# A hybrid decoder layer on one core: gate weights, gate bias and second norm around the end of the expert loop

## The chip, the cores and the metric

The kernel runs on one core of a Trainium2 chip. The metric is the device time of one execution in microseconds (us). Of three runs of the kernel before, the median is 1200.3 us (1199.73 to 1201.92).

## The reference

For 256 tokens of width 1024 the layer computes a token mixer, a mixture of experts and a gated per-layer embedding:

```
h = layer_norm(ALPHA * x + mixer(x) @ w_out) * ln1_g + ln1_b
m = sum over the top 4 of 32 experts of gate_e * (swiglu(h @ w_up[e] + b_up[e]) @ w_down[e] + b_down[e])
h = layer_norm(ALPHA * h + m) * ln2_g + ln2_b
out = h + sigmoid(h @ w_ple_gate + b_ple_gate) * (p @ w_ple)
```

All of it is in float32, and all 32 experts' weights (12 MB each) are read from HBM.

## The kernel before

The order of all work is written by hand: each engine runs its instructions in the order in which the program issues them, and semaphores hold an instruction until its inputs have landed and its output's place is free.

**Slots.** Most of SBUF is 22 buffers ("slots") of 128 x 2048 float32. `take` pops the first slot of a free list, `give` appends one to it. Weights stream through the slots, 1 MB in each, in one fixed list: for expert e the eight row blocks of `w_up` (`up`), the four of `w_down` (`dn`) of the expert before in between, `w_ple` (`ple`) in expert 27, and after the last expert the four pieces of `w_ple_gate` (`pg`). SyncE issues these loads (L63) as slots come free. A new tile in a slot waits for everything that used the slot before, the loads of its former tile among them.

**Expert loop** (L1257 on). For each expert and each k of 8, `up_slot` multiplies a 128-row block; at k = 1 the transposes of the expert before (`mid`), at k = 2 its `down`, at k = 4 and 5 of even experts `scatter` adds two experts' results to `z`. Each expert has room for 64 tokens. Tokens beyond that go through `overflow`: a loop over extra blocks whose count is known only at run time, inside `tc.If(n > 0)` (L1104) after the last expert's up matmuls, with its own weight buffer `ov`. In the profiled execution the count is zero, so each engine jumps over the loop. Where it jumps, SyncE passes a row of semaphore events that make good for the loads that the loop would have issued.

**Per-layer embedding.** At the start of expert 27 `late_take` takes three slots (`pp`, `ple`, `gb2`) and loads `p` by GpSimd's queue. At the start of expert 28 `ple_mm` transposes it, lets VectorE copy the transposes (L1040), multiplies it with `w_ple` into `ple` (L1046), and spreads the second norm's scale and shift over all partitions into `gb2` with a matmul each (`bc_row`), copied out by ScalarE.

**After the loop.** `gate_high` rounds the gate weights to fp32r (`pgh`, L1159 on ScalarE and L1161 on GpSimd), `gate_low` makes the remainders (`pgl`, VectorE). The last pair's `scatter` and the second norm are done one 128-token half (t = 0, 1) after the other: `stats2`, `norm2` (a square root on ScalarE, L1180, two small VectorE instructions), `norm2_apply` (`zn`, L1187). `trans2` transposes `zn` and applies scale and shift on ScalarE (`h2h`, `pp`; L1212); `high2` and `low2` split the result. `gate_mm` accumulates high x high, high x low and low x high into five PSUM chunks (two of 512 columns for t = 0; 512, 256 and 256 for t = 1). Each chunk is opened by `gate_start`, a matmul that puts `b_ple_gate` into it: before, from row 67 of `bd` in float32 with four rows (L1229). `scale2` applies scale and shift to the residual copy (GpSimd for t = 0, VectorE for t = 1), and `finish` does sigmoid, product, sum and output for a chunk.

Of the kernel before, what the change touches and what calls it, by code (L numbers as in the profile page):

```python
# [10 lines left out]
BF = mybir.dt.bfloat16  # L11
# [3 lines left out]
OP = mybir.AluOpType  # L15
# [32 lines left out]
class Stream:  # L48
# [25 lines left out]
    def give(self, *names, keep=0):  # L74

        self.slots.keep += keep
        for name in names:
            self.slots.free.append(self.slots.held.pop(name))
        self.pump()
# [3 lines left out]
def hybrid_layer(ctx, tc, x, p, w_in, conv_w, conv_b, lru_w_r, lru_b_r, lru_w_i, lru_b_i, lru_lambda,  # L83
# [55 lines left out]
    iota32 = cp.tile([128, NE], F32, name="iota32")  # L139
    tri = cp.tile([128, 128], F32, name="tri")  # L140
    one = cp.tile([128, 1], F32, name="one")
    epsc = cp.tile([128, 1], F32, name="epsc")
    fold = cp.tile([128, NE], F32, name="fold")
    foldb = cp.tile([128, NE], BF, name="foldb")
# [28 lines left out]
    V.memset(one, 1.0)  # L173
    ones = one.to_broadcast([128, 128])
    V.memset(epsc, EPS)
    V.memset(wglr, 0.0)
    G.memset(wgt, 0.0)
    make_identity(nc, ident)
# [850 lines left out]
    def late_take():  # L1029
        late["pp"] = take("pp", (2, 4, T))  # L1030
        late["ple"], late["gb2"] = take("ple", (2, D)), take("gb2", (2, D))
        G.dma_start(late["pp"][:, 0, 0:2], p[0, 0].rearrange("(t p) c -> p t c", p=128))  # L1032

    def ple_mm():
        ple, gb2, pt2, pTt = late["ple"], late["gb2"], late["pp"][:, 0, 0:2], late["pp"][:, 1, 0:2]
        o = pt("b", [128, 2, T], "ppT")
        for kk in range(2):
            for t in range(2):
                PE.transpose(o[:, kk, t * 128:(t + 1) * 128], pt2[:, t, kk * 128:(kk + 1) * 128], ident)
        V.tensor_copy(pTt, o)  # L1040
        w = st.get(("ple", 0))
        for t in range(2):
            for dh in range(2):
                o = pt("c", [128, 512], "pl")
                for kk in range(2):
                    PE.matmul(o, lhsT=pTt[:, kk, t * 128:(t + 1) * 128], rhs=w[:, kk, dh * 512:(dh + 1) * 512], start=(kk == 0), stop=(kk == 1))  # L1046
                A.activation(ple[:, t, dh * 512:(dh + 1) * 512], o, AF.Copy)
        st.done(("ple", 0))
        for r in range(2):
            for dh in range(2):  # L1050
                A.activation(gb2[:, r, dh * 512:(dh + 1) * 512], bc_row(1 + r, dh), AF.Copy)
# [43 lines left out]
    def overflow(n):  # L1095
        ov = take("ov", (2, 1024))
        ctr = mw.tile([128, 1], F32, name="ctr")
        sc = mw.tile([128, 8], F32, name="osc")
        V.memset(ctr, -1.0)

        def dot(a, o):
            V.scalar_tensor_tensor(tmo, a, 1.0, sel, op0=OP.mult, op1=OP.mult, accum_out=o)

        with tc.If(n > 0):  # L1104
            with tc.For_i(0, n, 1):
                V.tensor_scalar(ctr, ctr, 1.0, None, op0=OP.add)
                V.tensor_scalar(sel, sta, ctr, None, op0=OP.is_le)
                V.scalar_tensor_tensor(sel, cum, ctr, sel, op0=OP.is_gt, op1=OP.mult)
                dot(iota32, sc[:, 0:1])
                V.tensor_copy(ti[:, 1:2], sc[0:1, 0:1])  # L1110
                er = nc.values_load(ti[0:1, 1:2], min_val=0, max_val=NE - 1, engines=[mybir.EngineType.SP])
                dot(sta, sc[:, 1:2])
                V.tensor_tensor(sc[:, 1:2], ctr, sc[:, 1:2], op=OP.subtract)
                V.tensor_scalar(sc[:, 1:2], sc[:, 1:2], 64.0, 64.0, op0=OP.mult, op1=OP.add)
                for t in range(2):
                    dot(posb[:, t, :], sc[:, 2 + t:3 + t])
                    V.tensor_tensor(sc[:, 2 + t:3 + t], sc[:, 2 + t:3 + t], sc[:, 1:2], op=OP.subtract)
                    dot(gate[:, t, :], sc[:, 4 + t:5 + t])
                dot(fold, sc[:, 6:7])
                selb = mw.tile([128, C], BF, name="selb")  # L1120
                V.tensor_copy(selb, sc[:, 6:7].to_broadcast([128, C]))
                oh = mw.tile([128, 2, 4, C], F32, name="oh", tag="oh")[:, :, 0]
                for t in range(2):
                    V.tensor_scalar(oh[:, t], iota64[:, 0, :], sc[:, 2 + t:3 + t], None, op0=OP.is_equal)
                xo = ov[:, 1, 0:512].rearrange("p (k c) -> p k c", k=KD)
                for k in range(KD):
                    gather_k(oh[:, :, None, :], xo, 0, k)
                gu = up_start(selb, "b")

                def wload(src):  # L1130
                    w = ov[:, 0]
                    SP.dma_start(w, src)
                    return w

                for k in range(KD):
                    for a in range(2):
                        w = wload(w_up[0, bass.ds(er, 1), k * 128:(k + 1) * 128, a * 1024:(a + 1) * 1024].rearrange("o p c -> p (o c)"))
                        up_mm(gu, xo[:, k, :], w, k == KD - 1, (a,))
                aT = act_T(swiglu(gu, mo2), mo2)
                se = scatter_mat(lambda i, t: (sc[:, 2 + t:3 + t], sc[:, 4 + t:5 + t]),  # L1140
                                 mw.tile([128, 4, T], F32, name="x1", tag="x1")[:, 0])
                o = pt("b", [128, 512], "dn")
                dnv = w_down[0].rearrange("e (q p j) c -> e q j p c", p=128, j=2)
                for q in range(4):
                    for j in range(2):
                        w = wload(dnv[bass.ds(er, 1), q, j].rearrange("o p c -> p (o c)"))
                        down_mm(o, aT, q, w.rearrange("p (j c) -> p j c", j=1), (j,))
                y_evac(o, 1)
                for t in range(2):
                    scatter(se, t, slice(64, 128))  # L1150
        give("ov")

    def gate_high(i, *ens):

# [18 lines left out]
    def stats2(t):  # L1173
        for hf in range(2):
            stats(z, sb2, t, hf)
        V.bn_aggr(mv2[:, t, 0:2], sb2[:, t, :, :])
# [49 lines left out]
    def gate_start(tag, *chunks):  # L1226
        for t, c0, c1 in chunks:
            o = pgs[t, c0, c1] = pt(tag, [128, c1 - c0], "pg")
            PE.matmul(o, lhsT=ident[64:68, 67:68].to_broadcast([4, 128]), rhs=bd[64:68, c0:c1], start=True, stop=False)  # L1229

    def gate_mm(i, j, *chunks):

# [22 lines left out]
    for e in range(NE):  # L1255
        g = e // 4
        for k in range(KD):  # L1257
            if k == 0:
                if e == 8:
                    z_init()  # L1260
                if e == PLE - 1:
                    late_take()
                if e == PLE:
                    ple_mm()

            if (e, k) in ((0, 6), (0, 7), (2, 2)):
                hold(1)
            if k == 4 and e == PLE - 2:
                hold(3)
            if k == 7 and e % 4 == 2 and e < NE - 4:  # L1270
                hold(1)
            if (e, k) == (0, KD - 1):
                mo = take("mo", (4, 512))
            if (e, k) == (2, 4):
                z = take("z", (2, D))
            up_slot(e, k)
            if e == 0 and k == 1:
                gates()
            if e and e % 2 == 0 and k in (4, 5):
                scatter(PAIR[e // 2 - 1], k - 4, first=(e == 2))  # L1280
            if e and k == 1:
                mid(e - 1, mo)
            if e and k == 2 and e < NE - 1:
                down(e - 1)
            if (e, k) == (NE - 1, 5):
                gate_start("a", *c0)
            if (e, k) == (9, 6):
                blocks = overflow_count()
            if e == 0 and k < KD - 2:
                gather_k(oh, x1[0], 0, k + 2, 2)  # L1290
            if e == 1:
                if k == 0:
                    x1.append(take("x1b", (2, KD, 2 * C))[:, 0])
                gather_k(oh, x1[1], 2, k, 2)
            if e % 4 == 3 and e < NE - 1:
                if k == 0:
                    oh = gather_start(g + 1)
                if k % 2:
                    gather_mm(oh, XE[g + 1], k // 2)
            if e % 4 == 3 and k == KD - 1:  # L1300
                give(f"xe{g}" if g else "x1b")
# [19 lines left out]
    norm2(0)  # L1321
    norm2_apply(0)
    scatter(PAIR[NE // 2 - 1], 1)
    gate_start("a", *c1[:2])
    gate_start("c", c1[2])
    stats2(1)
    trans2(0)
    whole2(0, 0)
    high2(0, 1)
# [20 lines left out]
    gate_mm(1, 0, *c1)  # L1350
    dump("z", z)
    scale2(1, 0, V)
    for n, c in enumerate(c0):
        gate_mm(0, 1, c)
        finish(n, *c)
    scale2(1, 1, V)
    for n, c in enumerate(c1):
        gate_mm(0, 1, c)
        finish((2 + n) % 4, *c)
# [30 lines left out]
```

## Time and profile before

| | |
|---|---|
| median of three runs | 1200.3 us |
| profiled execution, its own time | 1197.4 us |
| its span in the trace | 1195.7 us |
| TensorE busy | 1137.6 us (95%) |
| VectorE busy | 410.8 us (34%) |
| ScalarE busy | 250.8 us (21%) |
| GpSimd busy | 36.9 us (3%) |
| read from HBM | 445 MB, 373 GB/s over the span |

Times in the trace count from the span's start; PE is TensorE, DVE VectorE, ACT ScalarE, POOL GpSimd, SP SyncE, and a q behind an engine's name means its sequencer or DMA queue. In a timeline a row merges instructions of one kind that follow each other: start, time from the first one's start to the last one's end, engine, line, operation, output<-input, shapes and count; in brackets the idle time of the engine before it and what ended that. [...]

### The profile page before, as it was taken

To read this page: it belongs to the slowest core of one execution; us is meant where nothing else is said; L and a number is where in the kernel's file an instruction comes from. 1 tells how busy PE (TensorE), PEld (TensorE's weight loads), DVE (VectorE), ACT (ScalarE), POOL (GpSimd) and SP (SyncE) were. 2 spreads that over 40 slices of the span, in tenths; PEclk is the share of its full clock that TensorE was granted. 3 is DMA by queue.
4 is the path that set the end of the run, shared out by engine and by line. 5 is a ranking of instruction groups with operands and counts; after the bars stand their busy time and mean duration, and the time that the engine had idled before them with its cause. 6 is when DMAs were issued, how large, how long until landed. Compare 5 with 4: busy or idle time off the path is not lost. (4 is left out here: it accounts for less than half of the span.)

```text
span 1195.7 us, 14336 instructions
## 1 busy us (share of the span) xinstructions
PE 1137.6 (95%) x5886; PEld 550.4 (46%) x5886; DVE 410.8 (34%) x717; ACT 250.8 (21%) x404; POOL 36.9 (3%) x66
## 2 busy tenths in 40 slices
PE   8999999999999999999999988998899889999888
PEld 7999999643343343334333322332233223333236
DVE  8589687621212223231212121211121112121227
ACT  5784664411010010001000100100010001200033
POOL 6000000000000000000000000000000000000020
PEclk9999999999999998999999999999999999999988
DMA  9654865899999999999999999999999999999960
GB/s 337 218 168 143 278 252 205 351 352 421 414 426 426 427 426 427 426 426 427 426 426 427 426 428 426 427 426 427 427 426 427 427 426 426 427 427 427 426 268 36
DMA packets 92849, 447.16 MB, mean 374 GB/s; under 512 B 9345, under 2 KB 40423, under 8 KB 43532
## 3 DMA queue, kind: packets, MB, share of 16 engines
q1 hardware_dynamic: 91008, 444.69, 90.7%
q10 hardware_dynamic: 1340, 1.10, 0.4%
q8 instruction: 47, 0.77, 0.2%
q0 software_dynamic: 432, 0.42, 0.1%
q14 instruction: 22, 0.18, 0.0%
HBM read 445.13 MB, written 1.05 MB: 373 GB/s over the span
## 5 line engine op out<-in xcount | busy, mean ns | idle before, releaser
L935 PE MATMUL gu<-up,xe 128*64 128x512 f32 x1792 | 417.9, 602 | 17.6 <-DMA up<-in_w_up_dram 17.3
L962 PE MATMUL dn<-dn,mo 128*64 128x512 f32 x1024 | 232.3, 598 | 16.3 <-DMA dn<-in_w_down_dram 12.4
L935 PEld LDWEIGHTS gu<-up,xe 128*64 128x64 f32 x1792 | 119.5, 137 | 268.7 <-issue 202.0
L971 DVE COPY y2b<-dn 64x512 f32<-64x512 f32 x32 | 22.2, 694 | 391.8 <-ACT mo L973 391.8
L962 PEld LDWEIGHTS dn<-dn,mo 128*64 128x64 f32 x1024 | 71.7, 137 | 171.8 <-issue 134.3
L943 ACT ACTIVATE mo<-mo 128x512 f32<-128x512 f32 x32 | 20.1, 630 | 299.3 <-DVE mo L942 299.3
L973 ACT ACTIVATE mo<-dn 64x512 f32<-64x512 f32 x32 | 18.9, 591 | 267.9 <-PE dn L962 267.9
L999 DVE TENSOR_TENSOR z<-z,sc 128x512 f32<-128x512 f32 x60 | 41.2, 688 | 89.9 <-PE sc L995 89.9
L942 DVE TENSOR_SCALAR mo<-gu 128x512 f32<-128x512 f32 x32 | 22.1, 692 | 130.9 <-PE gu L935 112.2
L915 PE MATMUL ga<-oh,X 128*128 128x256 f32 x224 | 55.1, 389 | 0.0
L955 ACT ACTIVATE mo<-aTp 128x512 f32<-128x512 f32 x32 | 19.1, 598 | 150.9 <-PE aTp L954 150.9
L915 PEld LDWEIGHTS ga<-oh,X 128*128 128x128 f32 x224 | 40.3, 190 | 21.4 <-issue 8.1
L995 PE MATMUL sc<-mo,se 128*128 128x512 f32 x64 | 36.0, 645 | 0.7 <-ACT mo L973 0.7
L920 DVE TENSOR_SCALAR xe<-ga,parTB 128x256 f32<-128x256 f32 x28 | 15.2, 543 | 60.0 <-PE ga L915 60.0
L995 PE MATMUL sc<-y2b,se 128*128 128x512 f32 x64 | 32.7, 592 | 0.0
L918 ACT ACTIVATE xe<-ga,parTB 128x256 f32<-128x256 f32 x28 | 15.8, 565 | 74.8 <-PE ga L915 74.8
L935 PE MATMUL gu<-up,x 128*64 128x512 f32 x128 | 30.7, 603 | 0.0
L954 PEld LDWEIGHTS aTp<-ident,mo 128*128 128x128 f32 x128 | 17.7, 207 | 26.0 <-issue 25.2
L935 PE MATMUL gu<-up,x1b 128*64 128x512 f32 x128 | 29.5, 597 | 0.0
L293 PE MATMUL acc<-wo,yhl 128*128 128x512 f32 x96 | 23.5, 398 | 0.8 <-DVE wo L262 0.8
L1032 POOL DMA_DIRECT2D pp<-in_p_dram x1 | 0.8, 842 | 746.4 <-DMA up<-in_w_up_dram 746.4
L944 DVE TENSOR_SCALAR mo<-gu 128x512 f32<-128x512 f32 x32 | 22.1, 691 | 5.2 <-PE gu L935 5.2
(340 smaller groups left out, 1195.3 us busy)
## 6 DMA issues: line engine op xcount, KB each, us to landing
up<-in_w_up_dram SPq DMA_DIRECT2D x256, 1024.0 KB
dn<-in_w_down_dram SPq DMA_DIRECT2D x128, 1024.0 KB
v<-in_w_in_dram SPq DMA_DIRECT2D x4, 1024.0 KB
ma<-in_w_in_dram SPq DMA_DIRECT2D x4, 1024.0 KB
ga<-in_w_in_dram SPq DMA_DIRECT2D x4, 1024.0 KB
go<-in_w_in_dram SPq DMA_DIRECT2D x4, 1024.0 KB
mb<-in_w_in_dram SPq DMA_DIRECT2D x4, 1024.0 KB
wo<-in_w_out_dram SPq DMA_DIRECT2D x4, 1024.0 KB
```

The source lines that it names most:

```text
L293: PE.matmul(o, lhsT=l(k)[i], rhs=r(k)[j], start=first and m == 0, stop=last and m == len(n) - 1)
L915: PE.matmul(o, lhsT=X[:, t, k * 128:(k + 1) * 128], rhs=oh[:, t], start=(t == 0), stop=(t == 1))
L935: PE.matmul(gu[a][64 * hf:64 * hf + 64, :], lhsT=xk, rhs=w[:, (a - parts[0]) * 1024 + hf * 512:(a - parts[0]) * 1024 + hf * 512 + 512], st ...
L942: V.tensor_scalar(gc, gu[0], LIM, None, op0=OP.min)
L943: A.activation(sg, gc, AF.Sigmoid, scale=1.702)
L944: V.tensor_scalar(uc, gu[1], LIM, -LIM, op0=OP.min, op1=OP.max)
L955: A.activation(aT, o, AF.Copy)
L962: PE.matmul(o[64 * dh:64 * dh + 64, :], lhsT=aT[:, 2 * c + j, hf * 64:hf * 64 + 64], rhs=w[:, j - js[0], dh * 512:(dh + 1) * 512], start=( ...
L971: V.tensor_copy(dst, src)
L973: A.activation(dst, src, AF.Copy)
L995: PE.matmul(o, lhsT=se[rows, t * 128:(t + 1) * 128], rhs=(y2b if dh else mo[:, 3])[rows], start=True, stop=True)
L999: V.tensor_tensor(z[:, t, dh * 512:(dh + 1) * 512], z[:, t, dh * 512:(dh + 1) * 512], o, op=OP.add)
```

## The change

- `overflow` no longer gives `ov` back, so no later tile takes that slot.
- The gate bias is loaded by GpSimd's queue in `late_take` into partitions 0, 64 and 96 of a zeroed `gb2`. In expert 28, ahead of `ple_mm`, `gate_bias` makes three bfloat16 parts of it there: ScalarE rounds, VectorE subtracts the rounded part in the partitions from 64 (from 96) on, ScalarE rounds the rest. They stay in an unused part of the slot `pp`.
- `gate_start` becomes a bfloat16 matmul of ones (128 rows) with these parts.
- The first two gate starts move from expert 31 (k = 5) to after the last scatter. Eight matmuls of 128x256 on a buffer of zeros (`spin`) follow them, and the last gate start comes behind `stats2(1)`.
- `scale2(1, 1)` moves ahead of the first `finish`.

```diff
+    oneb = cp.tile([128, 1], BF, name="oneb")
...
+    V.memset(oneb, 1.0)
...
         G.dma_start(late["pp"][:, 0, 0:2], p[0, 0].rearrange("(t p) c -> p t c", p=128))
+        G.memset(late["gb2"], 0.0)
+        for i in (0, 64, 96):
+            G.dma_start(late["gb2"][i:i + 1, 0], b_ple_gate)
+
+    def gate_bias(n):
+
+        b, h = late["gb2"][:, 0], late["pp"][:, 0, 2:4].rearrange("p a b -> p (a b)").bitcast(BF)
+        late["pgb"] = h
+        if n == 0:
+            A.activation(h, b, AF.Copy)
+        else:
+            r = slice((0, 64, 96)[n], 128)
+            V.tensor_tensor(b[r], b[r], h[r], op=OP.subtract)
+            A.activation(h[r], b[r], AF.Copy)
...
                 for t in range(2):
                     scatter(se, t, slice(64, 128))
-        give("ov")
...
-            PE.matmul(o, lhsT=ident[64:68, 67:68].to_broadcast([4, 128]), rhs=bd[64:68, c0:c1], start=True, stop=False)
+            PE.matmul(o, lhsT=oneb.to_broadcast([128, 128]), rhs=late["pgb"][:, c0:c1], start=True, stop=False)
...
                 if e == PLE:
+                    for n in range(3):
+                        gate_bias(n)
                     ple_mm()
...
-            if (e, k) == (NE - 1, 5):
-                gate_start("a", *c0)
...
     scatter(PAIR[NE // 2 - 1], 1)
-    gate_start("a", *c1[:2])
+    gate_start("a", *c0, *c1[:2])
+    spin(8, "b")
+    stats2(1)
     gate_start("c", c1[2])
-    stats2(1)
...
     scale2(1, 0, V)
+    scale2(1, 1, V)
     for n, c in enumerate(c0):
         gate_mm(0, 1, c)
         finish(n, *c)
-    scale2(1, 1, V)
```

The order on ScalarE after the last expert's result is evacuated (`mo<-dn`), before, with the semaphores that each instruction waits for (HW0 to HW7 are the queues of SyncE's loads in turn; `pg_0` is on HW6, `pg_3` on HW1):

```order
L973 ACTIVATE mo_2838<-dn_6597 64x512 [waits PE_49]
L1159 ACTIVATE pgh0_6619<-pg_0_6315 128x1024 [waits DMAHW4_49,DMAHW6_49,DMAHW3_49,DMAHW1_49]
L1159 ACTIVATE pgh0_6619<-pg_0_6315 128x1024
L1159 ACTIVATE pgh1_6623<-pg_1_6321 128x1024 [waits DMAHW7_49,DMAHW0_49]
L1180 ACTIVATE mv2_2745<-mv2_2745,epsc_77 128x1 [waits DVE_49]
L1187 ACTIVATE zn_6618<-z_3044,mv2_2745 128x512 [waits DVE_49]
```

and in the changed kernel:

```order
L975 ACTIVATE mo_2840<-dn_6604 64x512 [waits PE_49]
L1174 ACTIVATE pgh0_6626<-pg_0_6326 128x1024 [waits DMAHW7_49,DMAHW6_49,DMAHW4_49]
L1174 ACTIVATE pgh0_6626<-pg_0_6326 128x1024
L1174 ACTIVATE pgh1_6630<-pg_1_6332 128x1024 [waits DMAHW7_49,DMAHW0_49]
L1195 ACTIVATE mv2_2747<-mv2_2747,epsc_78 128x1 [waits DVE_49]
L1202 ACTIVATE zn_6625<-z_3046,mv2_2747 128x512 [waits DVE_49]
```

The order of instructions is the same; the list of semaphores of the first copy has changed, since its output now lies in another slot.

The order on VectorE at the turn from expert 27 to 28, before (`gu` are the up results, `xe` the last gathered tokens, `ppT` the transposed embedding):

```order
L942 TENSOR_SCALAR mo<-gu_5819 128x512 [waits PE_49]
L944 TENSOR_SCALAR mo<-gu_5820 128x512 [waits DVE_49,PE_49]
L945 SCALAR_TENSOR_TENSOR mo<-mo 128x512 [waits DVE_49]
L946 TENSOR_TENSOR mo<-mo 128x512 [waits DVE_49,Activation_49]
L920 TENSOR_SCALAR xe_5834<-ga,parTB 128x256 [waits PE_49]
L1040 COPY pp<-ppT 128x512 [waits DMAHW4_49,DMAHW3_49,DMAHW6_49,DMAHW1_49,PE_49]
```

and in the changed kernel:

```order
L947 SCALAR_TENSOR_TENSOR mo<-mo 128x512 [waits DVE_49]
L948 TENSOR_TENSOR mo<-mo 128x512 [waits DVE_49,Activation_49]
L922 TENSOR_SCALAR xe_5840<-ga,parTB 128x256 [waits PE_49]
L1047 TENSOR_TENSOR gb_5819<-gb_5819,pp 64x1024 [waits DMAHW0_49,DMAHW3_49,DMASW6_49,DMAHW6_49,DMASW5_49,Activation_49]
L1047 TENSOR_TENSOR gb_5819<-gb_5819,pp 32x1024 [waits Activation_49]
L1056 COPY pp<-ppT 128x512 [waits DMAHW4_49,DMAHW6_49,DMAHW1_49,PE_49]
```

Two subtractions stand ahead of the copy, each behind a rounding on ScalarE. ScalarE's three roundings (L1044 and twice L1048) stand there between its last `xe` and the copies of `ple`.

## Rows read from the trace of the kernel before

**Rows 1.** The page: the busy share of the DMA engines in 40 equal slices

```profile
DMA  9654865899999999999999999999999999999960
```

**Rows 2.** Timeline of ScalarE after the last expert's result

```profile
1151.09 0.59 ACT L973 ACTIVATE mo<-dn 64x512 f32<-64x512 f32 x1 [4.76 <-PE dn L962]
1158.03 2.95 ACT L1159 ACTIVATE pgh<-pg 128x1024 fp32r<-128x1024 f32 x3 [6.35 <-SPq L1104]
...
1161.59 1.52 ACT L1187 ACTIVATE zn<-z,mv 128x512 f32<-128x512 f32 x2 [0.42 <-DVE mv L1182]
1164.51 1.51 ACT L1212 ACTIVATE h2h<-t,parTB 128x128 fp32r<-128x128 f32 x4 [1.40 <-PE t L1209]
```

**Rows 3.** Line 1104 by engine: count, ns min/median/max, first and last start

```profile
L1104 SPq EVENT_SEMAPHORE  x9: 17/17/17, 1146.1 to 1158.4; - x9
...
L1104 PEldq COMPARE_BRANCH  x1: 5802/5802/5802, 1128.4 to 1128.4; - x1
```

**Rows 4.** Timeline of GpSimd after the last expert's result

```profile
1153.17 1.03 POOL L1161 CAST pgh<-pg 128x1024 fp32r<-128x1024 f32 x1 [169.92 <-DMA pg<-in_w_ple_gate_dram]
...
1162.49 1.28 POOL L1192 TENSOR_TENSOR z<-zn,gb 128x512 f32<-128x512 f32 x1 [2.37 <-ACT zn L1187]
```

**Rows 5.** Timeline of VectorE after the last expert's result

```profile
1155.67 0.21 DVE L1176 BATCH_NORM_AGGREGATE mv<-sb 128x2 f32<-128x12 f32 x1
...
1167.44 0.54 DVE L1220 CAST h2h<-pp 128x512 fp32r<-128x512 f32 x1
...
1185.22 0.69 DVE L1241 TENSOR_TENSOR mo<-mo,ple 128x512 f32<-128x512 f32 x1 [1.77 <-ACT mo L1240]
...
1187.83 0.69 DVE L1242 TENSOR_TENSOR z<-z,mo 128x512 f32<-128x512 f32 x1
...
1192.34 0.42 DVE L1242 TENSOR_TENSOR z<-z,mo 128x256 f32<-128x256 f32 x1
```

**Rows 6.** Timeline of TensorE after the last scatter

```profile
1155.56 1.55 PE L1229 MATMUL pg<-bd,ident 4*128 4x512 f32 x4
1162.21 1.22 PE L1229 MATMUL pg<-bd,ident 4*128 4x256 f32 x2 [5.10 <-DVE z L999]
1163.36 1.97 PE L1209 MATMUL t<-ident,zn 128*128 128x128 f32 x8
1165.02 5.62 PE L1235 MATMUL pg<-pgh,h2h 128*128 128x512 f32 x16
1170.47 1.99 PE L1235 MATMUL pg<-pgh,h2l 128*128 128x512 f32 x8
```

**Rows 7.** Busy time by engine in two stretches, granted clock behind it

```profile
1166.00:1168.00 2.00, 2.00 (x6) 1.57 (x5) 1.93 (x6) 1.59 (x6) 1.62 (x2) 0.50 0.00 0
...
1170.00:1175.00 5.00, 5.00 (x27) 4.06 (x26) 3.38 (x5) 2.48 (x7) 0.00 (x0) 1.00 0.00 0
```

**Rows 8.** Timelines in experts 27 and 28; the last row from the DMA issues

```profile
1023.83 7.10 PE L1046 MATMUL pl<-ple,pp 128*128 128x512 f32 x16 [1.05 <-ACT xe L918]
...
1034.58 0.62 PE L862 MATMUL gu<-bub,foldb 128*64 128x512 bf16 x4
...
1023.05 0.68 DVE L1040 COPY pp<-ppT 128x512 f32<-128x512 f32 x1
...
982.40 0.84 POOL L1032 DMA_DIRECT2D pp<-in_p_dram  x1 [746.41 <-DMA up<-in_w_up_dram]
...
pp<-in_p_dram POOLq DMA_DIRECT2D x1, 256.0 KB, 7.2
```

**Rows 9.** TensorE's waits for `up` weights (us, times, longest) after 1096; its timeline

```profile
PE gu L935 <- DMA up<-in_w_up_dram: 1.6, 3, 0.6
...
1125.34 1.98 PE L1229 MATMUL pg<-bd,ident 4*128 4x512 f32 x4
...
1134.67 6.97 PE L962 MATMUL dn<-dn,mo 128*64 128x512 f32 x24 [3.77 <-PEq L1104]
...
1142.24 8.80 PE L962 MATMUL dn<-dn,mo 128*64 128x512 f32 x40
```

## The prediction

> **What bounds the kernel now.** I read the page first, then the chain of waits, then the timeline of one engine after another over the last 45 us, and last the stretch from expert 28 to the end of the expert loop. The page shows the DMA engines full from the ninth slice to the end of that loop [rows 1]: the weight stream sets the pace there, and a stall of TensorE costs only what has not been made up when the stream ends. The chain's only long piece is the gate matmuls close to the end. So the change is worth what it does between the last expert's result and the last output, less what its new work in expert 28 leaves over.
>
> In that stretch ScalarE is free at 1151.09 + 0.59 = 1151.68 and then sits for 6.35 us; its first weight copy (`pgh`, L1159) starts at 1158.03, and the idle time is put down to SyncE at L1104 [rows 2]. L1104 is the `tc.If` of the overflow blocks. SyncE goes through nine semaphore events there, from 1146.1 to 1158.4 [rows 3]: with no overflow block to run it stands in for the loads that it skips, queue after queue, and each event waits for the real loads before it, the gate weights at last. A slot whose last writer is `ov` is free only then. The copy needs none of the later weights: the second of the four had landed at 1153.17, when GpSimd's first cast started [rows 4], and the first stands before it in the stream. Behind the three copies stand the square root of the second norm, at 1158.03 + 2.95 = 1160.98, and `zn` (1161.59) [rows 2]. VectorE had the mean and variance at 1155.67 + 0.21 [rows 5] and TensorE did nothing from 1157.11 to 1162.21 [rows 6].
>
> **The change part by part.** All times are the profiled execution's.
>
> 1. *Slot not given back.* ScalarE's first copy waits for HW7, HW6 and HW4, no longer for HW1 and HW3 (its order is shown with the change); HW6 carries its own weight. Three copies take 2.95 [rows 2]: they run from 1151.7 to 1154.8, the third with a short wait for the second weight. The square root then waits for VectorE's 1155.88 and starts at 1155.9 instead of 1161.0: **-5.0**.
>
> 2. *Gate starts and spin.* [...] Moved by 5.0, `zn` ends at 1158.1. [...] The first four transposes (half of `zn`, from 1157.4) are then done when ScalarE gets free, and `h2h` starts at 1158.15: 6.36 ahead, so **-1.36** (-0.9 at the late end). The cast that opens the second half of the first gate block goes from 1167.44 [rows 5] to 1161.1. [...]
>
> 3. *Second `scale2` sooner.* Before, VectorE idled 1.77 until its first finish at 1185.22; after the second finish's last add (1187.83 + 0.69) it spent 1.3 on `scale2(1,1)` and then worked without a gap to 1192.76 [rows 5]. Now those two instructions of 0.69 fit into the 1.77. The next sigmoid was ready at about 1188.8; three finishes of two instructions each (2 x 0.69, then four of 0.4) end at about 1191.9: **-0.9**.
>
> 4. *Bias parts in expert 28.* They stand ahead of VectorE's copy of `ppT`, for which the `pl` matmuls wait. Before, the copy ran from 1023.05 for 0.68 and `pl` started at 1023.83 after 1.05 of idle time [rows 8]. Now ScalarE, VectorE, ScalarE, VectorE alternate ahead of it, each waiting for the one before: two copies of 1024 columns at 1.0 [rows 2] and two subtractions of 1024 columns, for which 0.69 for 512 [rows 5] gives 0.69 to 1.38. I take 1.3, for 512 columns cost 0.69 in each such row: `pl` starts 4.6 later (bounds 3.4 and 4.8). The bias rows come by GpSimd's queue, a memset and three small loads behind that of `pp`, which was issued at 982.4 and took 7.2 to land [rows 8]; four such one after another end at 1011, so nothing waits for them. An idle time like this also takes the clock down: after 3.77 idle, 24 down matmuls took 6.97, 0.29 each, and 40 later ones 0.22 each [rows 9], 1.7 in all. **Lag 4.6 to 6.3.**
>
> Made up before the loop ends: three waits for weights, 1.6 together, and the two fp32 gate starts in expert 31, 1.98 from 1125.34, which are gone [rows 9]. Left: 1.0 to 2.7. Behind them lies TensorE's jump over the overflow code, 5.80 from 1128.4 [rows 3], for which it idled 3.77 before L962 [rows 9]. If that time runs from when the sequencer reaches the branch, the lag vanishes in it; if it runs from the end of the matmuls, all of it stays. The row leans to the first (the branch began while up matmuls were still to run), but not with more of them queued: bounds 0 and 2.7, I take **+1.2**.
>
> On the branch the trace has that one row. [...]
>
> Sum: -5.0 - 1.36 - 0.67 - 0.9 + 1.2 = **-6.7**. 1197.4 becomes 1190.7; the profiled execution lies 2.9 under the median of the runs, so the forecast is 1200.3 - 6.7 = **1193.6**.
>
> **The rivals.**
>
> *A. GpSimd and VectorE hold each other up.* GpSimd's casts still wait for the weights, so its four `scale2` instructions (1.28 each [rows 4]) start at about 1160.2, 2.3 earlier only, while VectorE's `h2l` and first `pgl` move by 6 to 7, into them. If two or three of the four hold VectorE up for 1.3 each, it is 2.6 to 3.9 late; its wait for ScalarE absorbs 0.9 and the last `pgl` has some 1.4 to spare: about +1.0 to 1.6, so **1195.0**. Against it: a cast beside VectorE's adds from PSUM took its usual 1.03 [rows 4]. For it: no VectorE instruction with two SBUF inputs lay beside a GpSimd one there. [...]
>
> [...]
>
> *C. Expert 28's lag is kept whole.* Were the stream itself held up by late slots, only the gate starts would be won back: 6.3 - 1.9 in place of 1.2, **1196.8**. Against it: the DMA engines stayed full though TensorE spent 1023.8 to 1034.6 [rows 8] on work that frees no weight slot.
>
> *D. The wait is not the slot's.* If the copies are held by something else that ends at 1158, the 0.9 of part 3 and some 1.4 of part 2 stand against 1.2: **1199.2**, no change. The list of semaphores speaks against it.
>
> *E. Slower.* The bias rows land late, because the memset waits for its slot's last reader and the loads for one another, and expert 28 waits for them. The gain of 7.9 and the 3.5 made up cover a lag of 11.4, or 6.3 and a landing 5.1 after 1023; so it decides from 1028, or up to 3.8 later if the branch hides some. A landing at 1032 with nothing hidden: **1204**. Against it: the 1011 of part 4.
>
> **How the numbers follow.** Forecast 0.52 (its own range 1192.0 to 1195.0), A 0.16, B 0.13, C 0.08, D 0.06, E 0.05. A measurement of this kernel tells about 0.2%, 2.4 us, from no change. Faster means below 1197.9, which takes in the forecast, A, B and most of C; D and the rest of C are the same; E is slower: 0.85, 0.10 and 0.05. The range goes down to a lag that costs nothing and the upper ends of parts 2 and 3, 1191.0, and up past C, 1197.8.
>
> **What would show it.** Right: the first `pgh` copy right after ScalarE's last evacuation; the square root at VectorE's statistics; a granted clock of 1.00 through the first gate block; no `scale2` after a finish; `pl` 4 to 5 us later behind `xe`. Wrong: a copy that still waits for SyncE; `pgl` pieces longer than 1.3 or with gaps beside GpSimd; gaps in the DMA stream after expert 28; the down matmuls of expert 30 more than 3 us later.

## The result and the profile after

The changed kernel took 1209.44 us (median of 4 runs, 1209.2 to 1210.81), the kernel before beside it 1200.01 (4 runs, 1198.76 to 1201.92): a ratio of 1.008, 95% interval 1.0062 to 1.0097. It is 9.4 us slower; 6.7 less was forecast. The profiled execution has a span of 1208.0 and a time of 1209.67.

**Where the time went.** The middle of the expert loop first: windows of five experts, cut at ScalarE's evacuation of the down result (`mo<-dn`, the copy of an expert's result out of PSUM; start:end, length, busy time and count of PE, PEld, DVE, ACT, POOL, then the clock granted to TensorE as a share of its full speed, DMA share, GB/s). Before:

```profile
740.03:888.09 148.06, 137.31 (x590) 46.70 (x590) 32.23 (x58) 12.73 (x23) 0.00 (x0) 1.00 1.01 427
```

The same five experts after:

```profile
749.73:900.91 151.18, 137.96 (x590) 46.55 (x590) 32.22 (x58) 12.72 (x23) 0.00 (x0) 1.00 1.01 419
```

The same instructions, the same granted clock (1.00), a full DMA share (1.01) in both, and the last number differs: 427 and 419 GB/s. TensorE's busy time is 0.65 longer; the other 2.5 of the 3.1 us more are idle time, 2.3 of it waits for weights (13.0 against 10.7). An expert's weights are 12 loads of 1 MiB, 12.58 MB: at 427 GB/s 29.5 us, at 419 30.0, and the windows give 29.6 and 30.2. Followed along the loop, the same evacuation is late by 3.2 at the first expert (the runs e1, e5 and e6 below were 1.7 to 1.8 late there, whatever their slots), 4.9 at the fourteenth, 9.7 at the eighteenth, 14.4 at the twenty-seventh and 18.2 at the last. Up to the fourteenth TensorE sets the pace in both. Then the stream takes over in the changed kernel (TensorE is busy for 97% of 600 to 700 us), and after 700 us in the kernel before too (100% of 500 to 700, 91% of 700 to 800). The nine experts from the eighteenth evacuation to the twenty-seventh take 267.0 before and 271.7 after.

Nothing in the diff touches a weight load. What moved is their address. `oneb` is a tile of 2 bytes per partition in the constants pool, where it takes 32 (it lies at 36384, the next tile at 36416), and the pool of weight slots lies right behind: the first slot starts at byte 36864 before (9 x 4096) and at 36896 after, and all that follow it are moved with it. No trace holds an address: those given here and below stand in the built programs.

**The tail.** Timeline of ScalarE after (start, us, engine, line, operation, in brackets the idle time ahead and what ended it), the answer to [rows 2]:

```profile
1169.27 0.59 ACT L975 ACTIVATE mo<-dn 64x512 f32<-64x512 f32 x1 [4.76 <-PE dn L964]
1169.88 2.95 ACT L1174 ACTIVATE pgh<-pg 128x1024 fp32r<-128x1024 f32 x3
1174.10 0.30 ACT L1195 ACTIVATE mv<-mv,epsc 128x1 f32<-128x1 f32 x1 [1.26 <-DVE mv L1191]
1175.46 1.52 ACT L1202 ACTIVATE zn<-z,mv 128x512 f32<-128x512 f32 x2 [1.07 <-DVE mv L1197]
1177.03 1.51 ACT L1227 ACTIVATE h2h<-t,parTB 128x128 fp32r<-128x128 f32 x4
```

The 6.35 us for SyncE are gone; the copies follow the evacuation, and the square root waits for VectorE, as the prediction had it. TensorE, the answer to [rows 6], and its granted clock (third number) in two windows, to [rows 7]:

```profile
1173.64 0.92 PE L1244 MATMUL pg<-pp,oneb 128*128 128x512 bf16 x4
1174.40 1.04 PE L304 MATMUL spin<-bub 128*128 128x256 bf16 x8
1176.08 0.27 PE L1244 MATMUL pg<-pp,oneb 128*128 128x256 bf16 x1 [0.65 <-DVE z L1001]
1176.33 1.36 PE L1224 MATMUL t<-ident,zn 128*128 128x128 f32 x8
1177.54 2.11 PE L1250 MATMUL pg<-pgh,h2h 128*128 128x512 f32 x8
1181.00 2.08 PE L1250 MATMUL pg<-pgh,h2h 128*128 128x512 f32 x8 [1.35 <-DVE h2h L1235]
```

```profile
1174.00:1180.00 6.00, 4.95 (x29) 1.00 0.07 27
1180.00:1186.00 6.00, 4.63 (x22) 1.00 0.01 3
```

VectorE, to [rows 5], and GpSimd, to [rows 4]:

```profile
1179.96 0.89 DVE L1235 CAST h2h<-pp 128x512 fp32r<-128x512 f32 x1
1180.77 1.76 DVE L1238 TENSOR_TENSOR h2l<-pp,h2h 128x512 fp32r<-128x512 f32 x1
1182.46 0.15 DVE L1196 RECIPROCAL mv<-mv 128x1 f32<-128x1 f32 x1
1182.64 1.06 DVE L1197 SCALAR_TENSOR_TENSOR mv<-mv 128x1 f32<-128x1 f32 x1
1183.62 0.68 DVE L1238 TENSOR_TENSOR h2l<-pp,h2h 128x512 fp32r<-128x512 f32 x1
...
1198.38 0.69 DVE L1256 TENSOR_TENSOR mo<-mo,ple 128x512 f32<-128x512 f32 x1 [0.46 <-ACT mo L1255]
...
1204.60 0.42 DVE L1257 TENSOR_TENSOR z<-z,mo 128x256 f32<-128x256 f32 x1
```

```profile
1179.30 1.27 POOL L1208 TENSOR_TENSOR z<-z,gb 128x512 f32<-128x512 f32 x1
1180.52 1.46 POOL L1207 TENSOR_TENSOR z<-zn,gb 128x512 f32<-128x512 f32 x1
1182.06 1.62 POOL L1208 TENSOR_TENSOR z<-z,gb 128x512 f32<-128x512 f32 x1
```

From the last evacuation's start to VectorE's end the tail took 1205.02 - 1169.27 = 35.75, before 41.67: 5.92 won, not the 7.9 of the prediction's parts 1 to 3. The granted clock is 1.00 in both windows. Beside GpSimd's three operations the cast took 0.89, the first h2l 1.76 and the small L1197 1.06; the second h2l, after GpSimd's end, took 0.68.

**Expert 28 and the branch**, to [rows 8, 9 and 3]: the bias parts on ScalarE and VectorE, then TensorE, then the branch over the overflow code (count, ns min/median/max, start).

```profile
1038.09 1.05 ACT L1044 ACTIVATE pp<-gb 128x1024 bf16<-128x1024 f32 x1
1039.17 1.22 DVE L1047 TENSOR_TENSOR gb<-gb,pp 64x1024 f32<-64x1024 f32 x1 [0.79 <-ACT pp L1044]
...
1042.77 0.69 DVE L1056 COPY pp<-ppT 128x512 f32<-128x512 f32 x1
...
1043.56 9.06 PE L1062 MATMUL pl<-ple,pp 128*128 128x512 f32 x16 [5.53 <-issue]
```

```profile
1143.21 1.94 PE L937 MATMUL gu<-up,xe 128*64 128x512 f32 x8 [0.56 <-DMA up<-in_w_up_dram]
1145.71 1.94 PE L937 MATMUL gu<-up,xe 128*64 128x512 f32 x8 [0.56 <-DMA up<-in_w_up_dram]
1152.23 7.58 PE L964 MATMUL dn<-dn,mo 128*64 128x512 f32 x24 [4.59 <-PEq L1120]
```

```profile
L1120 PEldq COMPARE_BRANCH  x1: 6082/6082/6082, 1145.7 to 1145.7; - x1
```

`pl` starts after 5.53 of idle time, 1.05 before, and its matmuls take 1.96 more. Over the 24 down matmuls behind the branch the mean granted clock was 0.70, after 4.59 of idle time; before it was 0.77, after 3.77. TensorE waits for weights again at 1143.21, so it has caught up with the (slower) stream: nothing of the lag is left.

In sum: the last evacuation is 18.18 late, the tail 5.92 shorter, 12.26 in the traces. The profiled execution of before (1197.4) lay 2.6 under the 1200.01 and that of after 0.2 over its median, which leaves the 9.4.

### The profile page after: what moved, and what is told of

It is laid out like the page before. It is cut to its first block, busy times and chain, and to the rows that moved or that the text cites. A ratio compares the mean times of both kernels' runs of the same rounds, so it can differ in the third digit from the quotient of the medians.

```text
span 1208.0 us, 14362 instructions
## 1 busy us (share of the span) xinstructions
PE 1142.4 (95%) x5889; PEld 551.2 (46%) x5889; DVE 416.6 (34%) x720; ACT 254.0 (21%) x407; POOL 39.4 (3%) x70
## 3 DMA queue, kind: packets, MB, share of 16 engines
HBM read 445.14 MB, written 1.05 MB: 369 GB/s over the span
## 5 line engine op out<-in xcount | busy, mean ns | idle before, releaser
L937 PE MATMUL gu<-up,x1b 128*64 128x512 f32 x128 | 29.5, 597 | 0.0
```

What stands on the lines that cost most here:

```text
L937: PE.matmul(gu[a][64 * hf:64 * hf + 64, :], lhsT=xk, rhs=w[:, (a - parts[0]) * 1024 + hf * 512:(a - parts[0]) * 1024 + hf * 512 + 512], st ...
```

## Experiments

Theory T: the 32 bytes by which the weight slots moved slow the stream, and without that the change does about what the prediction's steps say. Rivals: the stream is slower for another reason (the new work in expert 28, the added instructions), and the tail's missing 2 us are the lag's.

**e1, the change with the slots put back.**

```
-    one = cp.tile([128, 1], F32, name="one")
-    oneb = cp.tile([128, 1], BF, name="oneb")
+    one2 = cp.tile([128, 2], F32, name="one")
+    one, oneb = one2[:, 0:1], one2[:, 1:2].bitcast(BF)[:, 0:1]
```

> The changed kernel, with the bfloat16 ones put into the unused bytes behind the float32 one, so that every slot starts again at the SBUF address that it has in the kernel before (36864 + n x 8192; in the changed kernel 32 bytes further). Theory A (the 32 bytes slow the weight stream): the stream is back at 427 GB/s, the up matmuls of expert 31 end as in the kernel before or up to 2.7 us later, and the kernel takes 1193 to 1197. Theory B (something else in the change slows the stream, such as the work of late_take or the slot that is not returned): still 420 GB/s and about 1209.

1193.82 us (1192.95 to 1194.82), ratio 0.9959 (0.9945 to 0.9972); the stream at 427 GB/s. Two names in one tile of the size that `one` had taken turn 9.4 us lost into 4.9 won (before beside it: 1198.7).

**e2, e3, e5, e6: the kernel before, with only the slots moved.** An unused tile ahead of them, of 32 bytes (`cp.tile([128, 8], F32, name="pad")`), of 64, of 128; and, in e6, the 256-byte tile `csb` taken out from ahead of them:

```
-    csb = cp.tile([128, 2, NE], F32, name="csb")
...
+    csb = ctx.enter_context(tc.tile_pool(name="cz", bufs=1)).tile([128, 2, NE], F32, name="csb")
```

> The kernel before with 32 unused bytes ahead of the slots, nothing else. Theory A: 420 GB/s and 1212 to 1218, that is the changed kernel's stream without its gain at the end. Theory B: 1200.

> The kernel before with 64 unused bytes ahead of the slots. If only the remainder modulo 64 counts, 427 GB/s and 1200; if the slots have to start at a multiple of 128 or more, 420 GB/s and 1212 to 1218. Theory B: 1200.

> The kernel before with 128 bytes of padding in the constants pool, unused: the weight slots start at 36992, a multiple of 128 and not of 256. Theory (the slots' start has to be a multiple of 256 bytes for the full rate; 32 bytes off gave 1215.96 us and 420 GB/s, 64 off gave 1212.0 and 421): still slow, 1208 to 1214 us, 419 to 422 GB/s through the experts' loop, 8 KB packets at a median of 312 to 313 ns. Rival (128 is enough): 1199 to 1202 us, 427 GB/s, 309 ns. Rival (the padding itself, or the place in the partition, costs in proportion to the shift): between 1216 and 1225.

> The kernel before with its 256-byte tile csb placed behind the weight slots and not ahead of them: the slots start at 36608, a multiple of 256 and not of 512. Theory (256 bytes): 1198 to 1202 us as before, 427 GB/s, packets at a median of 309 ns. Rival (512 or more is wanted, before and the aligned version both stood at 36864, a multiple of 4096): 1208 to 1216 us, 420 to 422 GB/s.

The packet times are those of the 49,276 packets of 8 KB in each trace (49,277 in e2), median and mean in ns; such a packet is one partition's row of a 1 MiB load.

| slots start at | off by | us | ratio to before | GB/s | packet |
|---|---|---|---|---|---|
| 36864 (before) | 0 | 1200.01 | | 427 | 309, 312.2 |
| 36896 (after) | 32 | 1209.44 | 1.008 (1.0062 to 1.0097) | 419 to 420 | 313, 317.7 |
| 36896 (e2) | 32 | 1215.96 | 1.0134 (1.0115 to 1.0153) | 420 | 313, 317.3 |
| 36928 (e3) | 64 | 1212.0 | 1.0104 (1.0086 to 1.0122) | 421 | 312, 316.5 |
| 36992 (e5) | 128 | 1212.08 | 1.0105 (1.0089 to 1.012) | 421 | 312, 316.3 |
| 36608 (e6) | 256 | 1199.55 | 1.0002 (0.9993 to 1.0012) | 427 | 309, 312.4 |

Windows of e5, and then of e6, over the same stretch:

```profile
700.00:900.00 200.00, 179.74 (x777) 58.71 (x773) 40.01 (x72) 16.63 (x30) 0.00 (x0) 1.00 1.01 421
```

```profile
700.00:900.00 200.00, 183.34 (x794) 61.96 (x792) 38.67 (x71) 17.10 (x31) 0.00 (x0) 1.00 1.01 427
```

The padding alone makes the kernel before slower; 128 bytes off are as bad as 64, and 256 cost nothing, though 36608 is no multiple of 512. So it is where the slots start, not the size of the shift and not the change's own work: 427 GB/s from the two starts that are multiples of 256 (36864 and 36608), 419 to 421 from those 32, 64 or 128 bytes past one, and none of these four kernels has an instruction that the kernel before lacks. The mean packet took 1.3 to 1.8% longer from the latter; what inside the DMA engines costs it no run shows.

**e4, the bias parts in expert 27** (`gate_bias` called at `(e, k) == (PLE - 1, 3)` in e1, not ahead of `ple_mm`).

> As e1_aligned, with the bias parts made in expert 27 at k = 3 instead of ahead of the embedding's matmuls in expert 28. If the lag of expert 28 is made up by the weight stream and hidden under the branch at the end of the loop, the same time as e1_aligned within 0.5 us; if 1 to 2.7 us of it are left, faster by that.

1194.28 us (1193.75 to 1195.65), ratio 0.9963 (0.995 to 0.9977): no different from e1. Without the lag TensorE reaches the branch sooner and idles longer behind it. TensorE in e1, then in e4:

```profile
1125.17 10.52 PE L937 MATMUL gu<-up,xe 128*64 128x512 f32 x48
1137.60 5.37 PE L964 MATMUL dn<-dn,mo 128*64 128x512 f32 x24 [1.91 <-PEq L1120]
```

```profile
1138.26 8.08 PE L964 MATMUL dn<-dn,mo 128*64 128x512 f32 x24 [4.31 <-PEq L1120]
```

In e1 the branch starts at 1131.2, takes 5.92, and runs beside TensorE's last up matmuls. After 1.91 of idle time the 24 down matmuls take 5.37, at a granted clock of 1.00 from 1138 to 1143; after 4.31 they take 8.08, and the clock of the same stretch of e4 is 0.50.

**e10, the slot alone** (the kernel before without `give("ov")`).

> The kernel before with one line of the change alone: the overflow block's slot isn't given back. No tile is added, so the weight slots stay where they were (427 GB/s). Theory (ScalarE's 6.35 us wait for SyncE at L1104 was the slot's, and goes): the first weight copy right after ScalarE's last evacuation, 4 to 5.5 us sooner in the tail; 1194.5 to 1196.0 us. Rival (the wait is another's and stays): 1199 to 1201.

1195.19 us (1194.14 to 1196.39), ratio 0.9965 (0.9952 to 0.9979). ScalarE, TensorE and a window with its granted clock:

```profile
1154.22 0.59 ACT L973 ACTIVATE mo<-dn 64x512 f32<-64x512 f32 x1 [4.76 <-PE dn L962]
1154.83 2.95 ACT L1158 ACTIVATE pgh<-pg 128x1024 fp32r<-128x1024 f32 x3
```

```profile
1160.38 0.69 PE L1228 MATMUL pg<-bd,ident 4*128 4x256 f32 x2 [0.15 <-DVE z L999]
1161.01 1.09 PE L1208 MATMUL t<-ident,zn 128*128 128x128 f32 x8
1162.21 3.45 PE L1234 MATMUL pg<-pgh,h2h 128*128 128x512 f32 x8
1166.34 2.08 PE L1234 MATMUL pg<-pgh,h2h 128*128 128x512 f32 x8 [0.68 <-DVE h2h L1219]
```

```profile
1163.00:1166.00 3.00, 2.67 (x7) 0.50 0.00 0
```

One line brings nearly all: the tail is 36.33 long, 5.34 under before's. (It lasts 41.4 to 42.2 in before, e2, e3, e5 and e6, which share it, and 35.2 to 36.5 in after, e1, e4 and e13; less than about 1 us between two tails shows nothing.)

**e11, e1 without the spins** (`spin(8, "b")` left out).

> The aligned version of the change without the eight spin matmuls ahead of the first transposes. [...] Rival (TensorE comes from the scatter and the gate starts with so little idle time that the clock holds without spins): 1193.3 to 1194.3, granted clock 1.00 over the first gate block.

1194.73 us (1193.24 to 1195.17), ratio 0.9957 (0.9944 to 0.9971), tail 35.75. TensorE and the same window:

```profile
1161.96 2.11 PE L1250 MATMUL pg<-pgh,h2h 128*128 128x512 f32 x8
1164.98 2.08 PE L1250 MATMUL pg<-pgh,h2h 128*128 128x512 f32 x8 [0.91 <-DVE h2h L1235]
```

```profile
1163.00:1166.00 3.00, 2.09 (x10) 1.00 0.03 5
```

Had the spins held the granted clock up, the author's estimate was 1194.6 to 1195.6 without them, and the time alone fits that, but e1 itself, run again as e13, took 1195.01. The trace decides for the rival: without spins the granted clock is 1.00 here, so the spins are worth nothing that can be seen. In e10, behind two four-row fp32 gate starts, the clock fell to 0.50 in this stretch, and the first eight gate matmuls took 3.45; in e11, behind four 128-row bfloat16 ones, it was 1.00, and they took 2.11. Form and number changed together, in one trace of each, so which of them did it is not shown.

**e12, e1 with the last `scale2` back behind the second finish.**

> The aligned version of the change with the last scale2 where it was before, behind the second finish. Theory (the move is worth 0.9 us, because VectorE works without a gap from there to its end): 1194.4 to 1195.2 us, the last VectorE instruction 0.6 to 1.2 later after down(30)'s start. Rival (the finishes wait for TensorE's last matmuls anyway): 1193.5 to 1194.1.

1194.99 us (1194.13 to 1196.26), ratio 0.9962 (0.9949 to 0.9975). In time this can't be told from e1. In the trace it can: from the start of VectorE's last four `pgl` pieces (1176.38) to its end (1191.62) 15.24, in e1 14.37 (1174.59 to 1188.96): 0.87, the prediction's 0.9.

**e7, e8, e9: GpSimd beside VectorE.** e7 is e1 without `scale2(0, 0, G)` and `scale2(0, 1, G)`, so that tokens 0 to 127 leave without the second scale and shift; e8 does them later, held back by a copy that reads VectorE's result; e9 does them on VectorE:

```
     high2(1, 0)
+    G.tensor_copy(warm, h2[0][:, 0, 128:129].bitcast(F32))   # e8
+    scale2(0, 0, G)
+    scale2(0, 1, G)
```

```
+    scale2(0, 0, V)          # e9
     high2(1, 0)
...
+    scale2(0, 1, V)
     scale2(1, 0, V)
     for n, c in enumerate(c0):
         gate_mm(0, 1, c)
         finish(n, *c)
+        if n == 0:
+            scale2(1, 1, V)
```

> The aligned version of the change (1193.82 us) without GpSimd's four operations of the second scale and shift of tokens 0 to 127 (that half of the output leaves unscaled): it prices the pair GpSimd/VectorE. Theory (they hold each other up: VectorE's h2l took 1.78 us beside GpSimd and 0.68 alone, the small L1197 1.06 and not 0.16): h2l back at 0.68, L1197 at 0.16 for t = 1, the second norm's zn about 2 us sooner, the last VectorE instruction 1 to 2 us sooner after down(30)'s start; 1191.5 to 1193.0 us. Rival (what VectorE gains is covered by TensorE and ScalarE): 1193.5 to 1194.2.

> The aligned version of the change with GpSimd's second scale and shift held back until VectorE has made the h2 high part of tokens 128 to 255, by a one-element copy on GpSimd that reads it (some 4.5 us later in the tail, all work kept). Theory: h2l and L1197 at 0.68 and 0.16, zn of t = 1 about 2 us sooner; GpSimd's four operations then stand beside L1182, L1238 and scale2(1) of VectorE and lengthen these, partly under TensorE's last 64 matmuls: 1192.0 to 1193.6 us, at best the time without the four operations. Rival (the cost only moves: VectorE is late for the last matmuls or for the first finish): 1193.8 to 1196.

> The aligned version of the change with the second scale and shift of tokens 0 to 127 on VectorE and not on GpSimd: the first half in VectorE's idle 1.18 us ahead of its h2 high part of tokens 128 to 255, the second half after the last pgl, and scale2(1,1) behind the first finish. Theory (GpSimd beside VectorE costs what leaving its four operations out gave back, 1193.82 to 1191.42; VectorE's own four cost some 0.2 in the idle stretch and 0.6 to 0.9 at the end): 1192.0 to 1192.9 us, and no VectorE row of the tail longer than its like elsewhere. Rival (VectorE is then the bound of the tail, all four of its 0.69 land on the path): 1193.8 to 1194.5.

e7 took 1191.42 us (ratio 0.9934, 0.992 to 0.9947; tail 34.11), e8 1197.03 (0.9977, 0.9967 to 0.9987; 38.52), e9 1192.71 (0.9942, 0.9928 to 0.9957; 34.47). VectorE in e9, the first h2l, L1197 and the second h2l, with no GpSimd operation beside them:

```profile
1164.61 0.69 DVE L1238 TENSOR_TENSOR h2l<-pp,h2h 128x512 fp32r<-128x512 f32 x1
1165.21 0.15 DVE L1196 RECIPROCAL mv<-mv 128x1 f32<-128x1 f32 x1
1165.40 0.16 DVE L1197 SCALAR_TENSOR_TENSOR mv<-mv 128x1 f32<-128x1 f32 x1
1165.48 0.68 DVE L1238 TENSOR_TENSOR h2l<-pp,h2h 128x512 fp32r<-128x512 f32 x1
```

In e8 they had these lengths too, but then the held-back operations fell on the next ones, and it took more than even its rival allowed. VectorE and TensorE in e8:

```profile
1172.96 3.48 DVE L1238 TENSOR_TENSOR h2l<-pp,h2h 128x512 fp32r<-128x512 f32 x2
...
1176.37 6.81 DVE L1182 TENSOR_TENSOR pgl<-pg,pgh 128x1024 fp32r<-128x1024 f32 x4
```

```profile
1182.10 0.49 PE L1250 MATMUL pg<-pgl,h2h 128*128 128x512 f32 x1 [0.63 <-DVE pgl L1182]
```

In e9 the same two h2l took 1.29 and the four `pgl` pieces 4.63: e8 lost 4.4 where TensorE waits for them, against about 2 won ahead (its `zn` of t = 1 came 11.82 after the last evacuation, in e1 14.16, in e13 13.46). e8's rival was right: the cost moved with GpSimd's operations to the VectorE instructions that they then stood beside.

**e13, e14: side by side.** e13 is e1 again, e14 is e9 without the spins.

> The aligned version of the change once more, beside e14 on the same chip. All theories: ratio to before 0.995 to 0.997, from ScalarE's last evacuation to the last VectorE instruction 35.7 to 36.6 us.

> The aligned version with all of the second scale and shift on VectorE and without the spin matmuls. Theory (GpSimd beside VectorE takes 1.2 to 2.0 us of the tail, the spins are worth nothing): 1.0 to 1.8 us under the aligned version run beside it, tail 34.2 to 34.7 us, granted clock 1.00 over the first gate block. Rival (the gap between the sum of the prediction, 6.7, and the 4.9 measured is the lag of expert 28 and no matter of the tail): within 0.5 us of the aligned version.

e13 took 1195.01 us (1194.21 to 1195.84; ratio 0.9963, 0.9949 to 0.9976; tail 35.82), e14 1192.87 (1192.53 to 1194.9; 0.9949, 0.9935 to 0.9963; tail 34.77). The intervals overlap. On one chip e14 lies 2.1 us lower in the median and 1.05 in the tail; e13's h2l took 1.77, its L1197 1.06 and its next three `pgl` pieces 4.58; e14's 0.68, 0.16 and 3.49. e9 and e14, 0.5 to 0.6% under before, are the fastest kernels with all of the work.

How VectorE is held up can be read from the first L1197, that of t = 0, which starts while GpSimd rounds gate weights in two casts of 1.01 each. VectorE and GpSimd in e1, then in e9:

```profile
1157.77 0.95 DVE L1197 SCALAR_TENSOR_TENSOR mv<-mv 128x1 f32<-128x1 f32 x1
1157.68 2.02 POOL L1176 CAST pgh<-pg 128x1024 fp32r<-128x1024 f32 x2 [1.40 <-SPq L1120]
```

```profile
1159.43 0.32 DVE L1197 SCALAR_TENSOR_TENSOR mv<-mv 128x1 f32<-128x1 f32 x1
1158.70 2.02 POOL L1176 CAST pgh<-pg 128x1024 fp32r<-128x1024 f32 x2 [1.40 <-PE sc L997]
```

It lasts three times as long in e1 and yet ends at the same point in both, 1.04 to 1.05 after the pair's start, when the first cast is over; so it does in e7, e8 and e14 (0.35, 0.60 and 0.61 long). In each of these its end is that of the GpSimd cast that it met, within 0.04; with no GpSimd instruction beside it, as in before, it took 0.16.

## Why the prediction was wrong

The step that failed is the conclusion of its first paragraph: "So the change is worth what it does between the last expert's result and the last output, less what its new work in expert 28 leaves over." The loop ahead of expert 28 was thereby put at nothing, without a reason. But the new tile `oneb` stands in the diff, and its 32 bytes moved the buffers of the very stream that the prediction called the bound. The term that the sum lacks measured 1.2% on the changed kernel (ratios 1.008 and 0.9959, after and e1), some 14.5 us, and 1.3% on the kernel before (e2), some 16: +9.4 where -6.7 was forecast. e1, e2 and e6 show that the offset is the cause. No rival had it; the slower one, E, was the bias rows' landing, and the bias parts began at 1038.09, right behind the transposes. The premise, "the weight stream sets the pace there", holds only from some 700 us on in the kernel before: full DMA engines alone do not show it, since they were full from 500 to 700 too, where TensorE was busy all the time.

Point by point, with the tail counted from ScalarE's last evacuation to VectorE's end (41.67 before):

- *Slot, -5.0*: right. e10's tail is 5.34 shorter, its time 4.6.
- *Gate starts and spin, -1.36 and -0.67*: counted twice, and no run shows the two terms. The -1.36 took the transposes to start at 1157.4, behind four starts and eight spins, by an estimate of the author's; after, these twelve took 1.80 (from 1173.64 to 1175.44). The -0.67 is what the second eight gate matmuls took more than the next eight before (2.66 and 1.99), put down to the clock, granted at 0.50 from 1166 to 1168. The first `h2h` came 13.42 after the last evacuation before, 7.48 in e10 and 7.11 to 7.90 in the kernels with the change (7.06 forecast). The slot alone took TensorE's long idle time away (5.10, in e10 0.15), and with it what the prediction had given to the starts: the transposes went from 1.97, at a granted clock of 0.50, to 1.09 and the second eight gate matmuls from 2.66 to 2.08, and e11 has 2.08 there too. What is left for the starts is the first eight, 3.45 down to 2.11, and behind these TensorE waits for VectorE's cast in e10 as in e11; `zn` of t = 1 came no sooner for it (13.97 in e10, 13.39 to 14.47 with the change and its `scale2` on GpSimd).
- *Second `scale2`, -0.9*: right, 0.87 in e12's trace.
- *Lag in expert 28, +1.2*: the late start of `pl` was sized right (4.6 forecast, 5.53 of idle time against 1.05). Nothing of it is left: e4, without it, is no faster, and from the evacuation of expert 27 to the last one pass 144.1 us in e1, 144.8 in e13 and 144.8 in e4 (before 144.1, e6 143.7, e10 145.7). Counted from its own start the branch took 5.80 to 6.08 in before, after, e1, e4, e13 and e14, beside matmuls still to run, as the prediction leant to, and behind the shorter idle time in e1 (1.91) the granted clock was 1.00, in e4 (4.31) 0.50.
- *Rival A*: it was real, and belonged in the sum and not beside it. Priced at 1.0 to 1.6; in the median it was 2.1 us (e13 and e14, side by side) and 2.4 (e1 and e7, which were not, and e7 has less work). The 1.05 between the tails of e13 and e14 lies within what equal tails differ by. Clear of that is `zn` of t = 1: 13.4 to 14.5 after the last evacuation in the seven traces with `scale2` there on GpSimd, 11.5 to 11.8 in e7, e8, e9 and e14. Beside GpSimd's operations h2l took 1.09 longer, three `pgl` pieces 1.09 and a VectorE operation on a single column 0.9. GpSimd's own operations took longer too: 1.27 to 1.28 before, up to 1.74 in e1. What makes the two hold each other up no run shows.
- *Rivals B (a lower granted clock through the first gate block), C and D*: out. The granted clock was 1.00 from 1174 to 1186, the lag was made up, and the wait was the slot's.

So with the slots aligned the change came to -4.9 (e1) and -4.5 (e13), not -6.7. The tail's 5.1 to 6.5 (e1 and e4) in place of 7.9 carries that; e14, which takes GpSimd out of VectorE's way, gets to -6.7. Between e2 and the changed kernel, both 32 bytes off, lie 6.5 us (ratios 1.0134 and 1.008), so how much the change is worth by itself is known only as 4.5 to 6.5. That e1's 1193.82 meets the forecast of 1193.6 so closely is in part luck: before measured 1198.7 beside it, and a tail that won less than forecast met a lag that cost less.

## What to carry to other kernels

Where a DMA stream is the bound, look at the start addresses of its buffers before and after a change: any tile added to a pool ahead of them moves them all, and here 32 bytes cost more than the whole change won. Put small constants into a tile that exists, or behind the streaming buffers. And when one wait goes, count again what its idle time had caused (here transposes that took 1.97 at a granted clock of 0.50, and 1.09 in e10) before giving the same gain to another edit.

## What the hardware did that was not expected

- A stream of 8 KB packets into SBUF ran at 427 GB/s with buffers that start at 36864 or 36608, multiples of 256 bytes, and at 419 to 421 with buffers 32, 64 or 128 bytes past 36864, with a full DMA share (1.01) in both.
- A VectorE operation on one column per partition, 0.16 us alone (before, e9), took 1.05 to 1.06 beside a GpSimd operation of 512 columns (after, e1, e4, e11) and 0.32 to 0.95 beside a GpSimd cast of 1.01 (after, e1, e4, e7, e8, e9, e14), and in each of these ended within 0.05 of the end of that GpSimd instruction.
- Eight extra matmuls ahead of the transposes did nothing for the granted clock, which was 1.00 with them (e1) and without (e11). In e10, with less idle time than e11 (0.15 against 0.88 ahead of the last gate start) but two four-row fp32 starts in place of four 128-row bfloat16 ones, it fell to 0.50 behind the transposes.
- TensorE's taken branch over the overflow code took 5.80 to 6.08 us, that of the other engines 0.05 to 0.08.
